# Two attention entries on TensorE: the scheduler's order against source order, with half-steps between single projection units

## The chip, the core and the metric

The kernel runs on one core of one Trainium2 chip. The metric is device time in microseconds (us) of one execution, as the median of several. TensorE (PE) multiplies matrices, with weight loads (PEld) that overlap it; VectorE (DVE), ScalarE (ACT) and GpSimd (POOL) work on its results, and SyncE (SP) issues most DMAs. Each engine takes its instructions in order and waits on semaphores for the others.

## The reference

One encoder layer is applied to two request groups with the same weights: a prompt of 1024 tokens and a sample of 512 tokens, width 1024. Cut to what matters here:

```python
h = rms_norm(x, norm_g) * (1.0 + scale) + shift
rq, rk, rv, rg, aq, ak, av, ag = jnp.split(h @ w_in, splits, axis=-1)
# (A) chunkwise retention on rq, rk, rv (4 heads of 128)
# (B) attention: 8 query heads, 2 key/value heads of 64
aq = axial_rope(rms_norm(aq, q_norm_g), ...)
ak = axial_rope(rms_norm(ak, k_norm_g), ...)
p = softmax(q @ k.T / 8)          # every query sees every key of its group
att_out = p @ v
mixed = concat([ret_out * silu(rg), att_out * silu(ag)]) @ w_out
y = x + gate * mixed
```

Everything is float32, and the products that need it are made of three matmuls on high and low parts.

## The kernel before, in words

`sequence(r, nt, first)` (from L316) handles one group. It is called for the sample first (tile names with s, `nt` = 4 tiles of 128 tokens, `first` true), then for the prompt (names with p, `nt` = 8). In each it transposes and scales the inputs into a high part `hh` and a low part `hl`, projects and computes the four retention heads, projects keys, values and the first part of the queries (`kvq_units`, L431), and then enters attention.

**Projections.** `project` (L355) makes one token tile of a query projection out of 8 times `mm3` (L148): three matmuls of 128x256, on lines 149 to 151. `q_unit` (L405) is a pair of such tiles, 48 matmuls in one PSUM bank (tile `paq`), with a yield after the first 24, and then the work of the others on it: square on ACT (`qsq`, L414), sum (`qss`), rotary (`qt1` L380, four pieces `qt2` L387) on DVE, reciprocal root and sum on POOL (`r_q` L127, `qt1` L425), and the normalised queries `q` on DVE (L401, `q_finish`, one unit later). `q_rest` (L891) yields the units that are still missing when attention starts: for the sample one pair of units and then the gates (`gates`, L760, tiles `pag`, 24 matmuls of 128x512 each with a yield in the middle); for the prompt six units of 48 matmuls (`paqp03`, `paqp13`, then `paqp00`, `paqp10`, `paqp01`, `paqp11`; the first digit is the half of the heads, the second the pair of tokens).

**Attention** is written as steps for each tile of 128 queries:

- `prep_split` (L832) splits the queries into `Q1`, on ACT and DVE for the first tile and on POOL for the others; `prep_T` (L839) transposes them (8 transposes, tile `pq1`) and ACT copies them to `Q1T` (L847).
- Row maxima: `nat_head` (L851, sample) or `nat_pairs` (L858, prompt) multiply queries by keys (tiles `pn`) and DVE reduces them to `nm` (L856) or `nmh` (L869, 128x1024, eight a tile). `mid` joins them, `mid_t` (L883) transposes them (`pnm`) and DVE writes them as extra rows of `Q2T` (L887), whose other rows are copies of low parts (`fill_q2`, L871).
- Scores: `st_unit` (L913) makes a 128x1024 score tile `pT` from `Q1T` (L910) and `Q2T` (L921), ACT takes its exponential `p` (L924), and POOL or DVE adds it to the row sums `acc` (L929, L932).
- `pv_pair` (L934) multiplies two exponentials by the values into `po`, one bank that is held for the whole tile; `row_sums` (L949), `normalise` (L957), `gate_out` and `out_step` (L1004) finish a tile; the last makes the output product `py` from `w_out`, which `read_wo` (L900) loads back from DRAM.

**Rounds.** `at_round` (L1026) files each step under a round number and a priority in it; a tile has `nt` rounds, and steps that prepare it are filed in the rounds ahead of its own. `run_rounds_list` (L271) gives a flat list of the steps of a stretch of rounds.

**Order around the change.** The rest of attention, from round `turn` on, is written inside `tc.manual_schedule` for TensorE (L1103): there the source order is TensorE's order. The entry before it, rounds -100 to `turn`, is woven in with the missing projections by `weave` (L279): after each yield of a projection it issues as many attention steps as keep the two lists in proportion, `lead` shifts that proportion. This part stands outside the manual schedule, so a scheduler with its own timing model chooses the final order on every engine. For the prompt the entry is cut at round `PTURN`: the first part runs beside `paqp03` and `paqp13`, then the half of `hh` and `hl` that is done is released and its memory goes to `Q2T`, the exponentials and the rest.

**PSUM** has eight banks. In attention the prompt has three wide buffers of two banks (`pq1`, `pn`, `pT`, `pnm`, the row sums) and two single banks (`paq`, `po`, `py`); the sample has two wide ones and four single banks.

Of the kernel before, what the change touches and what calls it, by code (L numbers as in the profile page):

```python
# [33 lines left out]
OUTLAG = 0  # L34
WZ = 2
WOH = (0,1,3,4)
LEAD = 5
PLEAD = 3
PTURN = -7
KPOST = (1, 1)  # L40
PBUFS = (5, 6)
NATS = (1, 3, 5, 6)
# [38 lines left out]
def hybrid_layer_kernel(ctx: ExitStack, tc: tile.TileContext, a: dict, y_prompt: bass.AP, y_sample: bass.AP):  # L81
# [189 lines left out]
    def run_rounds_list(rounds, lo, hi):  # L271
        return [fn for rd in sorted(rounds) if lo <= rd < hi for _, fn in sorted(rounds[rd], key=lambda z: z[0])]

    def iter_steps(fns):
        for fn in fns:
            fn()
            yield
# [38 lines left out]
    def sequence(r, nt, first):  # L316
# [4 lines left out]
        with ExitStack() as sctx:  # L321
# [11 lines left out]
            hpair = nt // 4  # L333
            tps = list(range(hpair, 2 * hpair)) + list(range(hpair))
            order = [2 * tp + i for tp in tps for i in range(2)]
            kv = {}
            QPRE = hpair if first else 1
# [160 lines left out]
            with ExitStack() as rctx:  # L498
# [292 lines left out]
                prev = None  # L791
# [47 lines left out]
            def prep_T(t):  # L839
                d = st8[t]  # L840
                Q1 = d["Q1"]
                pq = wide(f"pq1{tg}{t}")
                for h in range(QH):
                    T.transpose(pq[:, h * P : (h + 1) * P].bitcast(F32R), Q1[:, h, :, :].rearrange("p a d -> p (a d)"),
                                identr)
                d["Q1T"] = ate.tile([P, QH, P], F32R, tag="Q1T", name=f"Q1T{tg}{t}", bufs=2)
                S.copy(d["Q1T"].rearrange("p h q -> p (h q)"), pq)  # L847
                d["nm"] = ate.tile([P, QH], F32R, tag="nm", name=f"nm{tg}{t}")
                d["nmh"] = ate.tile([P, 2, QH], F32, tag="nmh", name=f"nmh{tg}{t}") if ng > 1 else None
# [8 lines left out]
            def nat_pairs(t, v, n, prev):  # L858
                d = st8[t]
                pairs = (2 * v, 2 * v + 1)  # L860
                pns = [wide(f"pn{tg}{t}{pr}{n}") for pr in pairs]
                for pn, pr in zip(pns, pairs):
                    for i in range(2):
                        rows = slice(i * DH, (i + 1) * DH)
                        T.matmul(pn[:, i * 512 : (i + 1) * 512], d["Q1T"][rows, 2 * pr + i, :],  # L865
                                 kk[v][rows, n * 512 : (n + 1) * 512], start=True, stop=True)
                for pn, pr in zip(pns, pairs):
                    with tc.issue_after(prev["mid"].ins) if "mid" in prev else ExitStack():
                        V.tensor_reduce(d["nmh"][:, n, 2 * pr : 2 * pr + 2], pn.rearrange("p (i k) -> p i k", i=2), AX.X, ALU.max, negate=True)  # L869
# [156 lines left out]
            def at_round(rd, prio, fn):  # L1026
                rounds.setdefault(rd, []).append((prio, fn))

            for n, t in enumerate(order):
                b = n * per_  # L1030
                hb = b - per_
                prev = st8[order[0]] if n == 1 else {}
                if n:
                    at_round(hb - nt // 2, 8, lambda t=t: prep_split(t))
                    at_round(hb - 1, 6, lambda t=t: prep_T(t))
                if nt == 4:
                    for h in range(QH):
                        at_round(hb + h // 2, 4, lambda t=t, h=h, prev=prev: nat_head(t, h, prev))
                else:
                    for j, k in enumerate(NATS):  # L1040
                        at_round(hb + k, 4, lambda t=t, j=j, prev=prev: nat_pairs(t, j // 2, j % 2, prev))
                for v in range(2):
                    at_round(b - 2 + v, 7.5, lambda t=t, v=v: fill_q2(t, v))
                    at_round(b - nt // 2 if v == 0 else b - 1, 7, lambda t=t, v=v: mid(t, v))
                    at_round(b - 1 + v, 3.5 if v else 5, lambda t=t, v=v: mid_t(t, v))
                for u in range(nt):
                    at_round(b + u, 1, lambda t=t, u=u: st_unit(t, u))
                    if u % 2:
                        at_round(b + u + 1, 3, lambda t=t, u=u: pv_pair(t, u // 2))
                at_round(b + per_, 3.2, lambda t=t: row_sums(t))  # L1050
                at_round(b + per_, 8.5, lambda t=t: normalise(t))
                at_round(b + per_ + 1, 9, lambda t=t: gate_out(t))
                if t == final:
                    at_round(b + per_ - 2, 9, lambda t=t: gate_ret(t))
                    at_round(b + per_ + 1, 10, lambda: final_steps(0))
                    at_round(b + per_ + 2, 10, lambda: final_steps(4))
                    continue
                for u in range(16):
                    rd = b + per_ + 3 + u * nt // 16
                    at_round(rd if first else min(rd, nt * per_), 2 if rd < nt * per_ or first else 4, lambda t=t, u=u: out_step(t, u))  # L1060
# [8 lines left out]
            for j in range(8):  # L1069
                at_round(turn + j // 2, 6, lambda j=j: read_wo(j))  # L1070

            pools["q2"] = ate
            with ExitStack() as bctx:
                ra = run_rounds_list(rounds, -100, turn)
                if first:
                    pools["at"] = sctx.enter_context(pool(f"at{tg}", bufs=2, reuse_waits="tile"))
                    pb = bctx.enter_context(pool(f"pb{tg}", bufs=2, reuse_waits="tile"))
                    prep_split(order[0])
                    prep_T(order[0])
                    weave(itertools.chain(q_rest(pb, tps[hpair], hpair), gates(pb, "tg")), 4 * (nt // 2 - QPRE) + 8 * ng,  # L1080
                          iter_steps(ra), len(ra), LEAD)
                else:
                    nb = sum(len(rounds[rd]) for rd in rounds if rd < PTURN)
                    with pool(f"pb0{tg}", bufs=2, reuse_waits="tile") as pb:
                        prep_split(order[0])
                        prep_T(order[0])
                        weave(q_rest(pb, tps[QPRE], hpair - QPRE), 4 * (hpair - QPRE), iter_steps(ra[:nb]), nb + 1)
                    hpools.pop().release()
                    pools["q2"] = sctx.enter_context(pool(f"q2{tg}", bufs=1, reuse_waits="tile"))
                    pools["at"] = sctx.enter_context(pool(f"at{tg}", bufs=2, reuse_waits="tile"))  # L1090
                    pb = bctx.enter_context(pool(f"pb{tg}", bufs=2, reuse_waits="tile"))
                    weave(q_rest(pb, tps[hpair], hpair), 4 * hpair, iter_steps(ra[nb:]), len(ra) - nb, PLEAD)
                if first:
                    ln_tables()
            for p_ in reversed(hpools):
# [37 lines left out]
```

## Time and profile before

| | us |
|---|---|
| median of 3 runs | 983.63 (981.81 to 984.15) |
| profiled execution, its own time | 980.19 |
| its span, first to last instruction | 978.3 |
| PE busy in the span | 931.1 (95%) |
| DVE / ACT / POOL busy | 545.0 / 337.1 / 348.7 |

The profile is one execution, and around its span lie 1.9 us. TensorE is the engine with little idle time, and its mean granted clock over the span is 0.983 of the full one. The share of busy time says little about one stage, so the entries are read from stretches of a few microseconds and from timelines of each engine.

### The profile page before, as it was taken

To read this page: it belongs to the slowest core of one execution; us is meant where nothing else is said; L and a number is where in the kernel's file an instruction comes from. 1 tells how busy PE (TensorE), PEld (TensorE's weight loads), DVE (VectorE), ACT (ScalarE), POOL (GpSimd) and SP (SyncE) were. 2 spreads that over 40 slices of the span, in tenths; PEclk is the share of its full clock that TensorE was granted. 3 is DMA by queue.
4 is the path that set the end of the run, shared out by engine and by line. 5 is a ranking of instruction groups with operands and counts; after the bars stand their busy time and mean duration, and the time that the engine had idled before them with its cause. 6 is when DMAs were issued, how large, how long until landed. Compare 5 with 4: busy or idle time off the path is not lost. (4 is left out here: it accounts for less than half of the span.)

```text
span 978.3 us, 15472 instructions
## 1 busy us (share of the span) xinstructions
PE 931.1 (95%) x6177; PEld 755.2 (77%) x6177; DVE 545.0 (56%) x1006; ACT 337.1 (34%) x582; POOL 348.7 (36%) x312
## 2 busy tenths in 40 slices
PE   4879998999999899999999999999899999999998
PEld 3769898987566799999999988899554555555556
DVE  2465556675664493534435343445866767676743
ACT  3352233343544362122222232232233443344341
POOL 4233453464234282222212111155442434342330
PEclk9999999999999999999999999999798999999999
DMA  9964877322821621111101111200035001101111
GB/s 274 274 185 138 269 220 248 84 58 102 363 88 44 204 66 45 44 45 44 44 14 33 43 44 44 74 2 17 0 155 210 22 22 43 44 22 44 44 44 43
DMA packets 95684, 92.99 MB, mean 95 GB/s; under 512 B 23502, under 2 KB 84858, under 8 KB 92540
## 3 DMA queue, kind: packets, MB, share of 16 engines
q1 hardware_dynamic: 92876, 77.85, 25.9%
q0 software_dynamic: 2736, 14.16, 3.7%
q8 instruction: 48, 0.79, 0.4%
q14 instruction: 24, 0.20, 0.1%
HBM read 77.30 MB, written 14.68 MB: 94 GB/s over the span
## 5 line engine op out<-in xcount | busy, mean ns | idle before, releaser
L932 POOL TENSOR_TENSOR accp<-accp,pp 128x512 f32<-128x512 f32 x48 | 64.6, 1345 | 131.9 <-ACT pp L924 130.0
L924 ACT ACTIVATE pp<-pTp 128x1024 f32<-128x1024 f32 x64 | 65.7, 1026 | 129.8 <-PE pTp L921 114.2
L869 DVE TENSOR_REDUCE nmhp<-pnp 128x2 f32<-128x1024 f32 x64 | 76.7, 1219 | 10.2 <-PE pnp L865 10.0
L941 PE MATMUL pop<-pp,VVp 128*64 128x512 f32 x256 | 66.2, 640 | 0.0
L149 PE MATMUL pvgp<-wvgp,hhp 128*128 128x256 f32 x224 | 65.1, 291 | 0.0
L149 PE MATMUL pqkp<-wqkp,hhp 128*128 128x256 f32 x224 | 64.7, 289 | 0.0
L150 PE MATMUL pvgp<-wvgp,hhp 128*128 128x256 f32 x224 | 64.4, 287 | 0.0
L151 PE MATMUL pvgp<-wvgp,hlp 128*128 128x256 f32 x224 | 63.9, 285 | 0.0
L151 PE MATMUL pqkp<-wqkp,hlp 128*128 128x256 f32 x224 | 63.7, 285 | 0.0
L150 PE MATMUL pqkp<-wqkp,hhp 128*128 128x256 f32 x224 | 63.4, 283 | 0.0
L932 DVE TENSOR_TENSOR accp<-accp,pp 128x512 f32<-128x512 f32 x48 | 34.3, 715 | 40.3 <-ACT pp L924 40.0
L149 PE MATMUL pyp<-wo,Mhp 128*128 128x512 f32 (+1 forms) x136 | 51.8, 381 | 0.0
L150 PE MATMUL pyp<-wo,Mhp 128*128 128x512 f32 (+1 forms) x136 | 51.6, 379 | 0.0
L151 PE MATMUL pyp<-wo,Mlp 128*128 128x512 f32 (+1 forms) x136 | 51.5, 379 | 0.0
L910 PE MATMUL pTp<-Q1Tp,kkp 128*128 128x512 f32 x128 | 47.7, 455 | 0.2 <-DVE nmhp L869 0.2
L921 PE MATMUL pTp<-Q2Tp,k2p 68*128 68x512 f32 x128 | 44.0, 426 | 3.5 <-DVE Q2Tp L887 3.5
L149 PEld LDWEIGHTS pqkp<-wqkp,hhp 128*128 128x128 f32 x224 | 43.0, 192 | 0.0
L150 PEld LDWEIGHTS pqkp<-wqkp,hhp 128*128 128x128 f32 x224 | 43.0, 192 | 0.0
L151 PEld LDWEIGHTS pqkp<-wqkp,hlp 128*128 128x128 f32 x224 | 42.9, 192 | 0.0
L149 PEld LDWEIGHTS pvgp<-wvgp,hhp 128*128 128x128 f32 x224 | 42.9, 191 | 0.0
L150 PEld LDWEIGHTS pvgp<-wvgp,hhp 128*128 128x128 f32 x224 | 42.8, 191 | 0.0
L151 PEld LDWEIGHTS pvgp<-wvgp,hlp 128*128 128x128 f32 x224 | 42.8, 191 | 0.0
(458 smaller groups left out, 2764.2 us busy)
## 6 DMA issues: line engine op xcount, KB each, us to landing
wo<-wod SPq DMA_DIRECT2D x16, 1024.0 KB, 14.8
wa<-in_w_ada_dram SPq DMA_DIRECT2D x16, 512.0 KB, 6.2
wod<-woz POOLq DMA_DIRECT2D x8, 1024.0 KB, 6.4
gr<-in_w_ada_dram SPq DMA_DIRECT2D x16, 256.0 KB, 5.1
xn<-in_x_prompt_dram SPq DMA_DIRECT2D x8, 512.0 KB, 6.9
xrp<-in_x_prompt_dram SPq DMA_DIRECT2D x8, 512.0 KB, 3.5
out_dram<-xrp POOLq DMA_DIRECT2D x7, 512.0 KB, 2.9
xs<-in_x_sample_dram SPq DMA_DIRECT2D x4, 512.0 KB, 6.3
```

What stands on the lines that cost most here:

```text
L149: T.matmul(out, lh, rh, start=first, stop=False)
L150: T.matmul(out, lh, rl, start=False, stop=False)
L151: T.matmul(out, ll, rh, start=False, stop=last)
L869: V.tensor_reduce(d["nmh"][:, n, 2 * pr : 2 * pr + 2], pn.rearrange("p (i k) -> p i k", i=2), AX.X, ALU.max, negate=True)
L910: T.matmul(pT[:, i * 512 : (i + 1) * 512], kk[v][:, kb], st8[t]["Q1T"][:, hs, :].rearrange("p h q -> p (h q)"), start=True, stop=False)
L921: T.matmul(pT[:, i * 512 : (i + 1) * 512], k2[v][:, kb], d["Q2T", v].rearrange("p h q -> p (h q)"), start=False, stop=True)
L924: d["exp", u] = S.activation(p, pT, AF.Exp)
L932: d["sum", v] = E.tensor_tensor(acc, acc, p[:, i * 512 : (i + 1) * 512], op=ALU.add)
L941: m = T.matmul(d["po"][v * DH : (v + 1) * DH, :], VV[:, 2 * kp + i, v, :], ps[v][:, i * 512 : (i + 1) * 512], start=(kp + i == 0), stop=(2 ...
```

## The change

The two attention entries are put inside the manual schedule for TensorE, so their source order holds there. The attention steps of an entry are no longer a flat list but go by whole rounds: `iter_rounds` yields once after all steps of a round, and `weave` alternates such half-steps with single yields of the projections. `prep_T` of the first tile becomes the first half-step. The first tile's row maxima are filed one round apart (`k if n else j`), and the three constants of the proportion are set anew.

```diff
@@ -34,9 +34,9 @@
-LEAD = 5
-PLEAD = 3
-PTURN = -7
+LEAD = 3
+PLEAD = 0
+PTURN = -2
@@ -1038,7 +1038,7 @@
                     for j, k in enumerate(NATS):
-                        at_round(hb + k, 4, lambda t=t, j=j, prev=prev: nat_pairs(t, j // 2, j % 2, prev))
+                        at_round(hb + (k if n else j), 4, lambda t=t, j=j, prev=prev: nat_pairs(t, j // 2, j % 2, prev))
@@ -1069,27 +1069,34 @@
+            def iter_rounds(lo, hi, before=()):
+                for fn in before:
+                    fn()
+                    yield
+                for rd in sorted(rounds):
+                    if lo <= rd < hi:
+                        for fn in run_rounds_list(rounds, rd, rd + 1):
+                            fn()
+                        yield
+
             pools["q2"] = ate
-            with ExitStack() as bctx:
-                ra = run_rounds_list(rounds, -100, turn)
+            with tc.manual_schedule(engines={mybir.EngineType.PE}), ExitStack() as bctx:
                 if first:
                     pools["at"] = sctx.enter_context(pool(f"at{tg}", bufs=2, reuse_waits="tile"))
                     pb = bctx.enter_context(pool(f"pb{tg}", bufs=2, reuse_waits="tile"))
                     prep_split(order[0])
-                    prep_T(order[0])
                     weave(itertools.chain(q_rest(pb, tps[hpair], hpair), gates(pb, "tg")), 4 * (nt // 2 - QPRE) + 8 * ng,
-                          iter_steps(ra), len(ra), LEAD)
+                          iter_rounds(-100, turn, [lambda: prep_T(order[0])]), nt + turn + 1, LEAD)
                 else:
-                    nb = sum(len(rounds[rd]) for rd in rounds if rd < PTURN)
                     with pool(f"pb0{tg}", bufs=2, reuse_waits="tile") as pb:
                         prep_split(order[0])
-                        prep_T(order[0])
-                        weave(q_rest(pb, tps[QPRE], hpair - QPRE), 4 * (hpair - QPRE), iter_steps(ra[:nb]), nb + 1)
+                        weave(q_rest(pb, tps[QPRE], hpair - QPRE), 4 * (hpair - QPRE),
+                              iter_rounds(-100, PTURN, [lambda: prep_T(order[0])]), nt + PTURN + 1)
                     hpools.pop().release()
...
-                    weave(q_rest(pb, tps[hpair], hpair), 4 * hpair, iter_steps(ra[nb:]), len(ra) - nb, PLEAD)
+                    weave(q_rest(pb, tps[hpair], hpair), 4 * hpair, iter_rounds(PTURN, turn), turn - PTURN, PLEAD)
```

Outside the two entries TensorE's order is the same in both kernels, and so is SP's. Three places in the prompt's entry show how the order moves (a number behind an underscore is a buffer's). First, TensorE at the transposes of the first tile's queries, tile 4; before, with the 48 matmuls of `paqp03` and 18 of `paqp13` ahead of them since the last keys:

```order
L149 MATMUL paqp13_7249<-wqp1_6961,hhp1_3519 128x256
L150 MATMUL paqp13_7249<-wqp1_6961,hhp1_3519 128x256
L151 MATMUL paqp13_7249<-wqp1_6961,hlp1_3521 128x256
L844 MATMUL pq1p4_7163<-identr_65,Q1p4_7160 128x128 x8
L149 MATMUL paqp13_7249<-wqp1_6961,hhp1_3519 128x256
```

and now, with the first 24 matmuls of `paqp03` ahead:

```order
L151 MATMUL paqp03_7176<-wqp0_6656,hlp1_3524 128x256
L844 MATMUL pq1p4_7201<-identr_65,Q1p4_7165 128x128 x8
L865 MATMUL pnp400_7214<-kkp0_6628,Q1Tp4_7210 128x512 x2
L865 MATMUL pnp410_7215<-kkp0_6628,Q1Tp4_7210 128x512 x2
L149 MATMUL paqp03_7176<-wqp0_6656,hhp1_3522 128x256
```

The transposes stand 42 projection matmuls earlier, and the first row maxima, which stood behind all of `paqp10`, follow them directly. Second, DVE at the extra rows of tile 4 (`nmhp4` are its row maxima, `Q2Tp40` its second operand for the scores); before:

```order
L401 TENSOR_TENSOR qp0_7334<-qt1p10_7452,r_qp10_7462 128x2x256
L869 TENSOR_REDUCE nmhp4_7175<-pnp430_7487 128x2
L419 TENSOR_REDUCE qssp01_7597<-qsqp01_7595 128x8
L380 TENSOR_TENSOR qt1p01_7598<-paqp01_7506,Cp00_7327 128x512
L869 TENSOR_REDUCE nmhp4_7175<-pnp421_7494 128x2
L869 TENSOR_REDUCE nmhp4_7175<-pnp431_7495 128x2
L887 TENSOR_TENSOR Q2Tp40_7502<-pnmp40_7531,identr_65 4x512
```

and now:

```order
L387 TENSOR_TENSOR qt2p13_7344<-paqp13_7278,Sp06_7170 128x8x16 x4
L401 TENSOR_TENSOR qp3_7175<-qt1p13_7342,r_qp13_7352 128x2x256
L419 TENSOR_REDUCE qssp00_7450<-qsqp00_7448 128x8
L875 COPY Q2Tp40_7401<-Q1Tp4_7210 64x2x128
L887 TENSOR_TENSOR Q2Tp40_7401<-pnmp40_7404,identr_65 4x512
L875 COPY Q2Tp41_7421<-Q1Tp4_7210 64x2x128
L380 TENSOR_TENSOR qt1p00_7451<-paqp00_7376,Cp00_7368 128x512
```

The extra rows stood right behind the last row maxima of their tile; now the maxima are long done and the rows stand behind the sum `qssp00` of a projection unit. Third, TensorE between `paqp01` and `paqp11`; before, from the end of `paqp01` on:

```order
L865 MATMUL pnp430_7487<-kkp1_6626,Q1Tp4_7172 128x512 x2
L865 MATMUL pnp421_7494<-kkp1_6626,Q1Tp4_7172 128x512 x2
L865 MATMUL pnp431_7495<-kkp1_6626,Q1Tp4_7172 128x512 x2
L886 MATMUL pnmp40_7531<-identr_65,nmp4_7174 4x128
L844 MATMUL pq1p5_7534<-identr_65,Q1p5_7483 128x128 x8
L910 MATMUL pTp40_7551<-Q1Tp4_7172,kkp0_6625 128x512 x2
L921 MATMUL pTp40_7551<-Q2Tp40_7502,k2p0_6627 128x512 x2
L886 MATMUL pnmp41_7560<-identr_65,nmp4_7174 4x128
```

and now:

```order
L151 MATMUL paqp01_7573<-wqp0_6656,hlp0_3523 128x256
L910 MATMUL pTp45_7673<-Q1Tp4_7210,kkp1_6629 128x512 x2
L921 MATMUL pTp45_7673<-Q2Tp41_7421,k2p1_6631 128x512 x2
L865 MATMUL pnp520_7682<-kkp1_6629,Q1Tp5_7416 128x512 x2
L865 MATMUL pnp530_7683<-kkp1_6629,Q1Tp5_7416 128x512 x2
L149 MATMUL paqp11_7690<-wqp1_6964,hhp0_3521 128x256
```

Before, two score tiles, two more maxima and the first value product stand between these rows and `paqp11`, all without a projection; now four rows of attention do. In the sample's entry ScalarE runs the last gate's tanh and the table load (L307) ahead of the exponential of the first tile's last score tile, `ps23`, and not behind it.

## Rows read from the trace of the kernel before

**Rows 1.** The page, first part: busy us (share of the span) xinstructions.

```profile
PE 931.1 (95%) x6177; PEld 755.2 (77%) x6177; DVE 545.0 (56%) x1006; ACT 337.1 (34%) x582; POOL 348.7 (36%) x312
```

**Rows 2.** Stretches, prompt's entry: us, then PE PEld DVE ACT POOL busy, PEclk, DMA, GB/s.

```profile
690.00:695.00 5.00, 4.09 (x29) 2.95 (x27) 5.00 (x10) 0.60 (x1) 1.28 (x1) 1.00 0.00 0
695.00:700.00 5.00, 2.40 (x12) 2.02 (x13) 4.94 (x9) 0.92 (x1) 2.62 (x4) 0.65 0.00 0
700.00:705.00 5.00, 4.65 (x13) 2.09 (x12) 4.25 (x7) 2.14 (x3) 3.58 (x3) 0.50 0.00 0
705.00:710.00 5.00, 5.00 (x12) 1.59 (x11) 2.27 (x3) 1.02 (x1) 1.99 (x2) 0.50 0.00 0
...
725.00:730.00 5.00, 4.00 (x24) 2.02 (x20) 5.00 (x9) 1.92 (x5) 4.46 (x5) 1.00 0.99 413
730.00:735.00 5.00, 4.82 (x12) 1.70 (x14) 4.94 (x7) 3.09 (x4) 4.92 (x4) 0.56 1.00 423
735.00:740.00 5.00, 4.27 (x13) 1.10 (x9) 3.77 (x6) 2.65 (x4) 0.64 (x1) 0.75 1.02 429
740.00:745.00 5.00, 4.66 (x14) 2.03 (x14) 3.72 (x5) 1.76 (x3) 0.88 (x1) 0.66 1.01 418
```

**Rows 3.** Timeline of PE: start, us, engine, line, out<-in, count [idle before <-releaser].

```profile
697.82 1.23 PE L844 MATMUL pq1p<-identr,Q1p 128*128 128x128 f32 x8 [2.19 <-DVE nmhp L869]
```

**Rows 4.** Timeline of PE, DVE and ACT: the first tile's queries in the prompt's entry.

```profile
660.70 0.68 PE L149 MATMUL paqp<-wqp,hhp 128*128 128x256 f32 x1
...
665.40 0.69 DVE L401 TENSOR_TENSOR qp<-qt1p,r_qp 128x512 f32<-128x512 f32 x1 [2.88 <-POOL r_qp L127]
...
666.18 0.62 ACT L139 CAST Q1p<-qp 128x512 fp32r<-128x512 f32 x1 [4.30 <-DVE qp L401]
...
666.84 0.69 DVE L140 TENSOR_TENSOR Q1p<-qp,Q1p 128x512 fp32r<-128x512 f32 x1 [0.74 <-ACT Q1p L139]
...
669.01 0.80 PE L844 MATMUL pq1p<-identr,Q1p 128*128 128x128 f32 x8
...
669.84 1.01 ACT L847 CAST Q1Tp<-pq1p 128x1024 fp32r<-128x1024 f32 x1 [2.13 <-PE pq1p L844]
```

**Rows 5.** Timeline of PE and DVE: pieces of a projection unit and of row maxima.

```profile
661.46 0.28 PE L149 MATMUL paqp<-wqp,hhp 128*128 128x256 f32 x1
661.58 0.28 PE L150 MATMUL paqp<-wqp,hhp 128*128 128x256 f32 x1
...
712.58 0.73 PE L865 MATMUL pnp<-kkp,Q1Tp 64*128 64x512 f32 x4
...
718.88 0.73 PE L910 MATMUL pTp<-Q1Tp,kkp 128*128 128x512 f32 x2
...
676.16 0.67 DVE L419 TENSOR_REDUCE qssp<-qsqp 128x8 f32<-128x512 f32 x1
...
677.35 0.87 DVE L387 TENSOR_TENSOR qt2p<-paqp,Sp 128x128 f32<-128x128 f32 x4
...
688.14 2.35 DVE L869 TENSOR_REDUCE nmhp<-pnp 128x2 f32<-128x1024 f32 x2
```

**Rows 6.** Timeline of PE, then stretches (PE busy, PEclk, DMA, GB/s): a wait amid projections.

```profile
159.13 0.49 PE L739 MATMUL pos<-R1s,qd1s 128*128 128x128 f32 x2 [3.04 <-DVE qd1s L716]
...
161.00:162.00 1.00, 1.00 (x7) 0.50 0.74 201
...
164.00:165.00 1.00, 1.00 (x11) 0.99 0.97 352
```

**Rows 7.** A stretch of the sample's attention, columns as in rows 2.

```profile
285.00:290.00 5.00, 3.71 (x17) 2.65 (x16) 1.97 (x3) 1.84 (x4) 2.49 (x4) 1.00 0.33 108
```

**Rows 8.** Timeline of PE: the prompt's first output product.

```profile
746.46 0.40 PE L149 MATMUL pyp<-wo,Mhp 128*128 128x512 f32 x1
```

**Rows 9.** Timeline of PE and ACT: end of the sample's entry.

```profile
247.99 0.73 PE L910 MATMUL pTs<-Q1Ts,kks 128*128 128x512 f32 x2 [0.79 <-DVE Q2Ts L887]
...
246.92 1.28 ACT L307 ACT_TABLE_LOAD   x1
```

## The prediction

> **What bounds the kernel now.** I read the page's first part, then busy time in short stretches around both attention entries, then the timelines of TensorE, VectorE, ScalarE and POOL there. TensorE is busy 95% of the span [rows 1], so only two things can be won: time in which it waits, and time in which its granted clock is at the lower of its two levels (0.50, which is 1.2 GHz). The entry of the second attention is the place that has both. In the stretches of [rows 2] the busy column falls short of 5.00 by 0.91, 2.60, 0.35 and 0 (690 to 710) and by 1.00, 0.18, 0.73 and 0.34 (725 to 745): 6.1 us of idle. The clock column costs, as busy time times one minus the clock, 0.84 + 2.33 + 2.50 = 5.7 us in the first four stretches and 2.12 + 1.07 + 1.58 = 4.8 us in the last three. Together the entry holds 6.1 + 10.5 = 16.6 us over what its matmuls need at the full clock. The cause of the first half is seen in [rows 3]: TensorE has spent its projections, holds row-maximum matmuls only, and waits 2.19 us on VectorE, which reduces them. The first attention's entry has one wait worth a name, and it comes below; nearly all of the case is the second one.
>
> **The change, part by part.** The matmuls, and the work of the other engines, are the same in number; the order is what moves. So the sum is: idle and clock loss of before, 16.6 us, against those of the new order. I walk TensorE from 660.70 on, where the first unit of the remaining projections starts [rows 4] and everything ahead is unmoved. Units are half as long as they are in the code of before: 24 matmuls, 0.12 us apart [rows 5], 2.9 us, and then a piece of attention.
>
> *The first wait.* The transposes of the first tile's queries now stand behind 24 matmuls and no longer behind 66. The 24 end near 660.70 + 0.52 + 23 x 0.12 = 664.1 (the first of a kind takes some 0.5). But the queries come off a chain that the change leaves where it was: normalisation on VectorE at 665.40, ScalarE's high part at 666.18, VectorE's low part at 666.84 for 0.69 [rows 4]. TensorE waits until 667.5: **3.4 us**. Before, the transposes came at 669.01 and found the queries ready. Then the row maxima follow at once and need the transposed copy, which ends 1.84 us after the first transpose (669.01 to 669.84 + 1.01) and is handed over some 0.06 later; the eight transposes take 0.80 of that: **1.1 us**.
>
> *PSUM buffers.* Three wide buffers turn round. The fourth row-maximum tile waits for the reduction of the third, 1.13 us (two take 2.35 with overlap) plus a hand-over of some 0.25, and has two tiles, 0.73 us, ahead of it [rows 5]: 0.6. One score tile waits likewise for an exponential of 1.01 and has two maximum tiles ahead of it, 0.4. **1.0 us**.
>
> *The first scores.* On VectorE the copy and the maximum row of Q2Tp40 now stand behind qssp00, which needs ScalarE's square of a unit whose last matmul is the one just ahead of the scores. After that matmul: a 128x512 pass of ScalarE (0.62), qssp00 (0.6), a copy (between 0.2 and 0.69, I take 0.2), the row (0.69) and hand-overs, 2.3 us, of which TensorE fills 0.5 with the first score pair: **1.8 us**.
>
> *The last bank.* From the first value product on, one of the two small banks is held by pop4, so paqp11 needs the bank of paqp01. Its release is 0.62 on ScalarE, then 1.2 for two VectorE passes (676.16 to 677.35), 1.13 for a reduction that stands between them, 0.8 for four rotary pieces [rows 5], and 0.25: 4.0 us. TensorE has a score tile (two pairs like that of 0.73, some 1.0 with overlap) and two maximum tiles (0.73) to do: **2.3 us**.
>
> *The end of the entry.* After the last projection the order is that of before, tile 5 without any output projection to fill it. The last unit's square, sum and rotary now stand ahead of both maximum rows of tile 5 on VectorE, and pnp610 waits for a reduction behind tile 4's normalisation. I walk 0.8 + 0.4 + 1.75 = **2.95 us**; bounds are the 2.25 that before has there [rows 2] and 4.
>
> New idle: 3.4 + 1.1 + 1.0 + 1.8 + 2.3 + 2.95 = 12.6 us.
>
> *The clock.* No row shows this order, so I bound it. The nearest row to the first wait is a wait of 3.04 us amid dense projections in the first sequence [rows 6]: there the clock then stood at 0.50 for some three us and was back at 164, since dense work followed. That is 1.7 us, and I take it, because 24 dense matmuls follow here too; the upper bound is the 5.7 us of [rows 2], where sparse work followed, the lower is 0. For the middle waits I take 0: 1.29 us of idle left the clock at 1.00 [rows 7]. For the end I take half of the 4.8 us, between 0 and 4.8. Sum 4.1 us.
>
> The Trainium skill ("TensorE: Matmul & The Clock Gate", section "A second HAM failure mode: psum-queue depth-cycling") speaks against this reading: a TensorE that idles briefly but often between groups, as it turns through PSUM banks, falls to its lower clock and comes back again and again. The stretch of [rows 7] does not show that for one such wait, and no stretch of before has as many in a row as the new order; by that rule the sum would be some 5 us higher, three waits at 1.7 us each (third rival).
>
> Second entry: 12.6 + 4.1 - 16.6 = +0.1 us.
>
> *Loads.* The eight loads of the split w_out go out behind the last projection, which by the walk ends near 729, and move with it, as do the DMAs behind them on SP's queue. In [rows 2] the DMA share stands near 1.00 for 20 us, 2.5 us a load. The first product that needs one stood at 746.46 [rows 8]; it has over ten us of cover left, and later loads are needed slower than they come. Nothing. If that cover went, each microsecond would be lost in full.
>
> *First entry.* At most the wait of 0.79 us goes [rows 9]. But ScalarE now runs the last gate's tanh (0.62, a 128x512 pass) and the table load (1.28) ahead of the exponential (1.01, the 128x1024 pass of [rows 4]) whose buffer the next transposes need: 2.9 us, of which TensorE covers some 1.5. I take +0.4, between -0.8 and +0.6. The early moves of POOL's and VectorE's pieces (the second tile's split, Q2Ts copies) lie beside projections and cost nothing while those last; without that cover they would be late by their own 0.6 to 1.3 us.
>
> Total: +0.1 + 0.4 = **+0.5 us**. Against the profiled execution of 980.19 that is 980.7; the median of the three runs, 983.63, is 3.4 above that execution, so I give **984.1**. Within 0.3% (2.95 us) is about what a measurement here can't tell from no change.
>
> **The rivals.**
> 1. *The clock stays up.* Projections mixed in are just what [rows 2] lacked. If neither the first wait nor the end stage loses clock, the second entry is 12.6 - 16.6 = -4.0, total -3.6: **980.0**. For it: every stretch with projections has clock 1.00. Against it: the first wait is longer than the 3.04 us that did lower the clock. It decides if the granted clock is 1.00 from 730 on and lower for under two us near 667.
> 2. *The first wait costs as [rows 2] did.* After it come transposes, a second wait and row maxima before the 24 matmuls, so the half clock may hold for the 13 us that it held from 696 to 710: 5.7 us in place of 1.7, total +4.5: **988.1**. It decides if the clock is still 0.50 when paqp13 starts (about 677).
> 3. *Every bank wait lowers the clock.* Three middle waits (scores, buffer, last bank) at 1.7 us each: total +5.6, **989.2**. The skill's rule above would have it so; of the rows only [rows 3] has a 2 us wait with a fall, and it stood amid sparse work.
> That the order does not come out as written is excluded: it is read from the built program.
>
> **How the numbers follow.** Forecast, no change that can be told: 0.47. Rival 1: 0.26. Rival 2: 0.21. Rival 3: 0.06. The forecast's own range is from 981 to 987 by the bounds of the end stage and of the first entry. To hold 8 in 10 the range reaches past rival 1 by a microsecond of shorter waits and just past rival 2: 979.0 to 988.7. Faster 0.26, same 0.47, slower 0.27.
>
> **What would show it.** A wait of 3 to 3.5 us before the first tile's transposes near 664, released by VectorE's low part, with the clock at 0.50 in the next stretch; about 1.8 us before Q2Tp40's scores, 2.3 before paqp11; the stretch that was 695 to 710 without a clock below 0.9; the first output product of tile 4 within 2 us of 746.5; in the first entry about 1.5 us before the transposes, released by ScalarE. I am wrong in kind if the first tile's transposes do not wait, or if the first output product comes before 743 or after 750.

## The result and the profile after

The changed kernel takes **989.13 us** (median of 15 runs, 984.37 to 993.79), the kernel before 984.12 (15 runs, 976.52 to 988.82). The ratio is 1.0055 with a 95% interval of 1.0033 to 1.0077, so the change costs 5.4 us (3.2 to 7.6) where the prediction said +0.5. It lies outside the range and on the slower side.

The work is the same and TensorE is still what bounds it. First part of the page of the changed kernel, as [rows 1] (busy us, share of the span, instructions):

```profile
PE 930.5 (94%) x6177; PEld 758.3 (77%) x6177; DVE 546.9 (55%) x1006; ACT 336.9 (34%) x582; POOL 349.5 (35%) x312
```

TensorE's busy time is within 0.6 us of before and the span is 987.0 instead of 978.3. To see where the 8.7 us come from, the span is cut at rows that both traces have, and only three pieces differ. The **first entry** runs from the gate broadcast of the sample (L392) to its first output product (L149), the **second entry** likewise in the prompt, and the **boundary** from the prompt's first zero product (L517), where the sample's work is over, to the first `pqkp` projection.

| stretch, us | before | changed |
|---|---|---|
| first entry | 59.4 | 62.0 |
| boundary | 37.2 | 40.1 |
| second entry | 87.1 | 90.9 |

Each piece of the rest is equal within 0.4 us. The boundary will turn out not to be the change's; the two entries are. Timeline of TensorE in the changed kernel, its waits (start, us, engine, line, out<-in, count, idle before and its releaser):

```profile
201.44 0.38 PE L149 MATMUL paqs<-wqs,hhs 128*128 128x256 f32 x1 [0.67 <-ACT gates L393]
...
248.94 0.51 PE L844 MATMUL pq1s<-identr,Q1s 128*128 128x128 f32 x4 [1.66 <-ACT ps L924]
...
667.24 0.39 PE L149 MATMUL paqp<-wqp,hhp 128*128 128x256 f32 x1 [0.68 <-ACT gmod L393]
...
673.01 0.84 PE L844 MATMUL pq1p<-identr,Q1p 128*128 128x128 f32 x8 [2.63 <-DVE Q1p L140]
674.95 0.80 PE L865 MATMUL pnp<-kkp,Q1Tp 64*128 64x512 f32 x2 [1.10 <-ACT Q1Tp L847]
...
681.87 0.50 PE L865 MATMUL pnp<-kkp,Q1Tp 64*128 64x512 f32 x2 [0.86 <-DVE nmhp L869]
...
698.49 1.07 PE L921 MATMUL pTp<-Q2Tp,k2p 68*128 68x512 f32 x2 [2.30 <-DVE Q2Tp L887]
...
726.75 0.55 PE L149 MATMUL paqp<-wqp,hhp 128*128 128x256 f32 x1 [2.50 <-DVE qt2p L387]
...
741.10 0.73 PE L910 MATMUL pTp<-Q1Tp,kkp 128*128 128x512 f32 x2 [0.39 <-ACT pp L924]
742.34 0.73 PE L921 MATMUL pTp<-Q2Tp,k2p 68*128 68x512 f32 x2 [0.51 <-DVE Q2Tp L887]
...
751.05 0.50 PE L865 MATMUL pnp<-kkp,Q1Tp 64*128 64x512 f32 x2 [1.50 <-DVE nmhp L869]
...
755.49 0.39 PE L149 MATMUL pyp<-wo,Mhp 128*128 128x512 f32 x1
```

The waits that the prediction walked are all here, where it put them and nearly as long (the second entry starts 5.3 us later than in [rows 4], so 673.01 is 667.7 in the time of before). Two rows were not expected, those at 201.44 and 667.24. Stretches of one microsecond in the second entry (PE busy and its instructions, PEclk, DMA share, GB/s):

```profile
674.00:675.00 1.00, 0.05 (x2) 0.86 0.00 0
675.00:676.00 1.00, 1.00 (x4) 0.50 0.00 0
...
678.00:679.00 1.00, 1.00 (x10) 0.93 0.06 16
...
698.00:699.00 1.00, 0.51 (x2) 0.81 0.00 0
699.00:700.00 1.00, 1.00 (x5) 0.50 0.06 16
...
702.00:703.00 1.00, 1.00 (x10) 0.98 0.00 0
...
726.00:727.00 1.00, 0.25 (x1) 0.50 0.00 0
727.00:728.00 1.00, 1.00 (x6) 0.50 0.00 0
...
732.00:733.00 1.00, 1.00 (x4) 0.62 0.00 0
...
743.00:744.00 1.00, 1.00 (x5) 0.50 1.00 418
...
746.00:747.00 1.00, 1.00 (x6) 0.80 0.95 401
```

The clock falls to 0.50 (1.2 GHz) four times: after the first wait, after the wait for `Q2Tp40`, after the wait for the last bank and in the end stage. Busy time times one minus the clock, summed over stretches of 1 us, gives 1.6 + 1.6 + 3.0 + 1.7 = 7.9 us (8.0 with stretches that begin at the entry's own start). The last of the four stands behind two short waits, of 0.39 and 0.51 us, and none stands behind the 1.50 us wait at 751. The long fall of [rows 2] at 695 to 710 is gone, as forecast; in place of it and the two falls that before has behind it, near 730 and 740, there are four. By the same sums the second entry of before has 6.1 us idle and 11.0 of clock loss, the changed one 13.3 and 8.0: +4.2, against the 3.7 by which the stretch grew.

### The profile page after: what moved, and what is told of

Same layout as the page of the kernel before. It is cut to its first block, busy times and chain, and to the rows that moved or that the text cites. A ratio compares the mean times of both kernels' runs of the same rounds, so it can differ in the third digit from the quotient of the medians.

```text
span 987.0 us, 15467 instructions
## 1 busy us (share of the span) xinstructions
PE 930.5 (94%) x6177; PEld 758.3 (77%) x6177; DVE 546.9 (55%) x1006; ACT 336.9 (34%) x582; POOL 349.5 (35%) x312
## 5 line engine op out<-in xcount | busy, mean ns | idle before, releaser
L149 PE MATMUL pvgp<-wvgp,hhp 128*128 128x256 f32 x224 | 65.0, 290 | 0.0
L149 PE MATMUL pqkp<-wqkp,hhp 128*128 128x256 f32 x224 | 64.6, 288 | 0.0
L941 PE MATMUL pop<-pp,VVp 128*64 128x512 f32 x256 | 63.7, 619 | 0.0
L932 DVE TENSOR_TENSOR accp<-accp,pp 128x512 f32<-128x512 f32 x48 | 34.2, 712 | 37.4 <-ACT pp L924 37.1
L149 PE MATMUL pyp<-wo,Mhp 128*128 128x512 f32 (+1 forms) x136 | 51.8, 381 | 0.0
L910 PE MATMUL pTp<-Q1Tp,kkp 128*128 128x512 f32 x128 | 45.6, 438 | 0.8 <-ACT pp L924 0.8
L149 PEld LDWEIGHTS pqkp<-wqkp,hhp 128*128 128x128 f32 x224 | 43.0, 192 | 0.0
L149 PEld LDWEIGHTS pvgp<-wvgp,hhp 128*128 128x128 f32 x224 | 42.8, 191 | 0.0
```

The lines of the kernel that those rows point to most:

```text
L149: T.matmul(out, lh, rh, start=first, stop=False)
L910: T.matmul(pT[:, i * 512 : (i + 1) * 512], kk[v][:, kb], st8[t]["Q1T"][:, hs, :].rearrange("p h q -> p (h q)"), start=True, stop=False)
L932: d["sum", v] = E.tensor_tensor(acc, acc, p[:, i * 512 : (i + 1) * 512], op=ALU.add)
L941: m = T.matmul(d["po"][v * DH : (v + 1) * DH, :], VV[:, 2 * kp + i, v, :], ps[v][:, i * 512 : (i + 1) * 512], start=(kp + i == 0), stop=(2 ...
```

## The experiments

The table gives for each run the three stretches of its profiled execution, idle and clock loss in the second entry summed in the same way, and the ratio to the kernel before on the same chip.

| run | first | boundary | second | idle + clock | ratio (95%) |
|---|---|---|---|---|---|
| before | 59.4 | 37.2 | 87.1 | 6.1 + 11.0 | 1 |
| changed | 62.0 | 40.1 | 90.9 | 13.3 + 8.0 | 1.0055 (1.0033 to 1.0077) |
| e1 sample only | 61.9 | 38.6 | 86.2 | 7.1 + 9.0 | 1.0026 (1.0000 to 1.0052) |
| e2 prompt only | 59.4 | 39.6 | 92.4 | 13.4 + 9.5 | 1.0050 (1.0023 to 1.0077) |
| e3 wide first | 61.1 | 37.7 | 90.5 | 13.3 + 7.9 | 1.0054 (1.0030 to 1.0078) |
| e4 one unit later | 62.0 | 39.6 | 86.3 | 10.6 + 6.6 | 0.9996 (0.9969 to 1.0022) |
| e5 spread | 63.0 | 39.2 | 83.3 | 8.8 + 4.7 | 0.9957 (0.9933 to 0.9981) |
| e6 late value products | 62.0 | 37.0 | 85.5 | 9.6 + 6.6 | 0.9995 (0.9973 to 1.0016) |
| e7 transposes ahead | 61.0 | 37.8 | 90.6 | 13.4 + 7.9 | 1.0068 (1.0040 to 1.0096) |
| e8 mix | 59.4 | 39.2 | 76.8 | 5.3 + 1.7 | 0.9869 (0.9840 to 0.9899) |
| e9 before, late value products | 59.3 | 38.9 | 79.6 | 5.2 + 3.4 | 0.9913 (0.9884 to 0.9942) |
| e10 mix, wide first | 61.4 | 37.9 | 77.9 | 5.1 + 3.3 | 0.9911 (0.9879 to 0.9943) |
| e11 changed again | 64.5 | 38.6 | 89.7 | 13.4 + 6.5 | 989.42 us, one execution |
| e12 before again | 59.4 | 37.1 | 88.9 | 6.5 + 12.4 | 981.72 us, one execution |

**One entry at a time (e1, e2).** The block under `pools["q2"] = ate` exists twice, once as in the change and once as before, and `first` chooses:

```diff
-            with tc.manual_schedule(engines={mybir.EngineType.PE}), ExitStack() as bctx:
+            if first:
+                with tc.manual_schedule(engines={mybir.EngineType.PE}), ExitStack() as bctx:
...
+            else:
+                with ExitStack() as bctx:
+                    ra = run_rounds_list(rounds, -100, turn)
...
```

with the constants of each side (e2 has the two branches the other way round).

> New order in the first attention's entry only; the second entry has the code and the constants of before. Three stretches are read: first entry (gate broadcast of the sample, line 392, to its first output product, line 149; 59.4 us before, 62.0 in the changed kernel), boundary (first xTp transposes of the prompt's loading to its first pqkp projection; 36.8 and 39.6), second entry (gate broadcast of the prompt to its first output product; 87.1 and 90.9). Theory A (each entry loses by itself, the boundary differs from run to run): first entry 62.0, second 87.1, time about +2.6 us over before. Rival B (a later sample makes the boundary's transfers land later, so the boundary's 2.8 us belong to the change): boundary 39.6 here, time about +5.5 us. Rival C (the second entry is where it is lost): time within 1 us of before.

> New order in the second attention's entry only; the first entry has the code and the constant of before. Theory A: first entry 59.4 us, second 90.9, time about +3.7 us over before; the clock falls to 0.50 after the wait for Q2Tp40 and after the wait of the last bank as in the changed kernel. Rival B: the boundary stays at 36.8 here and time is +3.7 as well, so that this run and the one before it differ by the boundary. Rival C (all is lost in the first entry): time within 1 us of before.

Each entry loses by itself: +2.6 us (2.5 in the first entry's stretch; the interval of the time begins at 0) and +4.9 us (5.2 in the second's). The clock did not fall after the wait for `Q2Tp40` in e2, against its expectation. The boundary is 38.6 and 39.6, so it goes with neither side. e11 and e12 are the two kernels themselves, profiled once more:

> The changed kernel itself, profiled a second time, to tell what belongs to its order and what to one execution. If the fall of the clock after the wait for Q2Tp40 belongs to the order, the clock is at 0.50 after that wait here too; if it is the execution's, as the runs with the same order suggest, it may stay at 1.00 there, and the fall after the first wait lasts some seven us in its place. Under both the idle of the second entry is 13.3 us within 0.3, its clock loss 7.9 to 9.5, and the fall after the wait for the last bank is there. If the boundary belongs to the change it is 40.1 us again, if to the execution anything from 37 to 40.

> The kernel before, profiled a second time. If the boundary belongs to the change it is 37.2 us again; if to the execution, anything from 37 to 40. The second entry is 86 to 88 us with some 6 us of idle and 9 to 11 us of clock loss, the first entry 59.4.

What TensorE waits for at the boundary (engine, line, waited for: us in total, times, longest), in the kernel before:

```profile
PE p0p L149 <- ACT hhp L507: 3.5, 1, 3.5
```

in the changed kernel:

```profile
PE p0p L149 <- ACT hhp L507: 6.3, 1, 6.3
```

and in e11, the same kernel again:

```profile
PE p0p L149 <- ACT hhp L507: 4.7, 1, 4.7
```

In both kernels' first profiles ScalarE's `hhp` is released by the landing of the sample's last output DMA, in e11 by that of a weight load (`wvgp0r`). One kernel shows 4.7 and 6.3, and kernels with the first entry of before show 37.1 to 39.6 for the stretch. Over all 14 profiles it is 37.0 to 40.1 with no order that goes with the change. So the 2.8 us of the profiled pair are mostly one execution's. e11 missed one expectation: its clock loss is 6.5, below 7.9; and its first entry is 64.5 (below). e12 missed one too: its second entry is 88.9 with 12.4 us of clock loss, over 86 to 88 and 9 to 11. So the order of before has a second entry of 86.2 to 88.9 us (before, e1, e12), the new one 89.7 to 92.4 (changed, e2, e3, e7, e11). The ranges do not meet, and the means lie 3.4 us apart; e2's 5.2 is the difference of one pair of profiles.

**The first projection's bank (e3).**

```diff
-                pq = wide(f"pq1{tg}{t}")
+                pq = st8[t].get("pq") or wide(f"pq1{tg}{t}")
...
                     prep_split(order[0])
+                    st8[order[0]]["pq"] = wide(f"pq1{tg}{order[0]}")
```

(the second line stands in both entries).

> Changed kernel, but the wide PSUM buffer of the first tile's transposes is allocated before the projections' first bank, as in before; the transposes stand where the change puts them. Theory A (the first remaining projection waits for ScalarE's copy of the gate broadcast only because its bank is now the one of that broadcast): the 0.7 us wait after line 392 goes in both entries; the first entry is 1.0 us shorter (61.0), the second as long as it was (90.9), since the projection that starts earlier only waits longer for Q1p4 (2.6 becomes some 3.8). Rival D (the swap of banks is the whole of the loss, because it also makes the middle waits): first entry 59.4 and second 87.1. Rival E (nothing but the place of the wait changes): both as in the changed kernel.

Theory A held. With `prep_T` as a half-step, the projections' `bank` tiles are the first to be allocated in the new pool, and they get the banks of the gate broadcast, which ScalarE has yet to copy. In e3 these waits are gone and the first entry is 0.9 us shorter. The second entry stays, since its next wait takes the time over. TensorE's waits in e3's second entry:

```profile
PE pq1p L844 <- DVE Q1p L140: 3.5, 1, 3.5
PE pTp L921 <- DVE Q2Tp L887: 2.9, 3, 2.2
PE paqp L149 <- DVE qt2p L387: 2.6, 2, 2.5
```

The wait for `Q1p4` is 3.5 instead of 0.68 + 2.63.

**What else the first entry loses (e7).** On top of e3:

```diff
-                    at_round(hb - 1, 6, lambda t=t: prep_T(t))
+                    at_round(hb - 1, 0.9 if first and n == 2 else 6, lambda t=t: prep_T(t))
```

> Changed kernel with the wide buffer allocated first (as in the third run), and in the first entry the transposes of the third tile's queries stand ahead of the last score pair of the first tile, so that their buffer no longer hangs on the exponential behind the tanh and the table load. Theory A (that order on ScalarE is what the first entry still loses): the 1.66 us wait before these transposes goes and at most 0.8 us comes back at the next buffer, first entry 60 us against 61.1. Rival H (tanh, table load, exponential and copy are one chain on ScalarE and TensorE meets its end in any order): the wait stands before pTs30 or pnms30 instead, first entry 61 or more. Second entry as in the third run, 90.5.

Rival H held: 61.0 us. ScalarE in the changed kernel (timeline):

```profile
245.86 0.60 ACT L362 ACTIVATE tg_as<-pags 128x512 f32<-128x512 f32 x1 [3.81 <-PE pags L151]
246.48 1.28 ACT L307 ACT_TABLE_LOAD   x1
247.77 1.02 ACT L924 ACTIVATE ps<-pTs 128x1024 f32<-128x1024 f32 x1
```

This chain begins when the last gate's projection ends, and TensorE meets its end in whatever it does next. In e3 the wait was the 1.7 us before the transposes, in e7 it is split (TensorE's waits in e7):

```profile
PE pnms L886 <- ACT Q1Ts L847: 0.9, 1, 0.9
PE pTs L910 <- ACT ps L924: 0.7, 1, 0.7
```

The 1.66 us wait can also cost clock. In e1, e5 and e11 the granted clock stands at 0.50 after it (1.7, 1.7 and 3.4 us of loss), in the changed kernel's first profile, e3, e4 and e6 it does not. That is the 64.5 of e11 (stretches of 5 us):

```profile
249.00:254.00 5.00, 4.46 (x16) 0.56 1.01 426
254.00:259.00 5.00, 5.00 (x19) 0.75 1.01 428
```

**More ahead of the transposes (e4, e5).** e4 gives the second entry's first `weave` a lead of one unit; e5 deals its six half-steps out as 0, 1, 2, 3 behind the four units:

```diff
-                              iter_rounds(-100, PTURN, [lambda: prep_T(order[0])]), nt + PTURN + 1)
+                              iter_rounds(-100, PTURN, [lambda: prep_T(order[0])]), nt + PTURN + 1, 1)
```

```diff
+            def batches(it, sizes):
+                for k in sizes:
+                    for _ in range(k):
+                        next(it, None)
+                    yield
...
-                              iter_rounds(-100, PTURN, [lambda: prep_T(order[0])]), nt + PTURN + 1)
+                              batches(iter_rounds(-100, PTURN, [lambda: prep_T(order[0])]), (0, 1, 2, 3)), 4)
```

> Changed kernel, but the first half-step of the second entry stands behind 48 projection matmuls and not behind 24. Theory A (the wait for Q1p4 and the clock that falls after it are paid because there is too little ahead of the transposes): 24 matmuls are 2.9 us, the wait of 2.6 us before the transposes goes to under 0.5 and no stretch at 0.50 follows; of the 2.6 + 1.6 us some 2 to 4 come back, second entry 87 to 89 us. Rival F (the cover is only moved: the matmuls taken forward are missing at the later waits, which grow by as much): second entry 90 to 92. If the middle waits stay above 2 us the clock falls after each of them here too.

> Changed kernel, but the six half-steps of the second entry's first part are dealt out as 0, 1, 2 and 3 behind its four projection units, where the changed kernel has 2, 2, 1 and 1 and the run with one unit more ahead had 0, 3, 2 and 1. Theory A (waits come from half-steps that follow each other at once): the transposes find Q1p4 ready, the 1.1 us for the copy of Q1Tp4 lie beside 24 matmuls, and no wait of the first part reaches 1 us, so no stretch there stands at 0.50; with the wait for Q2Tp40 gone as in that run, the second entry takes 82 to 84 us, against 90.9 and 86.3. Rival F (cover is only moved): the row maxima that come later make the row for Q2Tp40 late, a wait of 2 us or more stands before the first score pair again and the clock falls after it: 86 to 88 us.

Theory A's mechanism held in both: 86.3 (4.6 under the changed kernel, and under the 87 to 89 expected) and 83.3 (7.6 under it). In e4 the wait for `Q1p4` is gone, and with it that for `Q2Tp40`, which drops from 2.3 to at most 0.5; but row maxima now follow each other at once and one waits 1.9 us. Behind it the clock falls after all (1.7 us of loss), where Theory A expected no such stretch. TensorE's longest waits in e4, then a stretch:

```profile
PE pnp L865 <- DVE nmhp L869: 4.6, 3, 1.9
PE paqp L149 <- DVE qt2p L387: 2.6, 2, 2.5
PE pnp L865 <- ACT Q1Tp L847: 1.1, 1, 1.1
...
679.00:680.00 1.00, 1.00 (x5) 0.50 0.07 16
```

In e5 the first part has no wait of 1 us and no stretch below 1.00; the last bank's wait of 2.5 us is left, and the clock falls after it.

**The last bank (e6, e8, e9).** The value products of the prompt's first tile, and with them its accumulator, move behind the start of the last projection unit:

```diff
-                        at_round(b + u + 1, 3, lambda t=t, u=u: pv_pair(t, u // 2))
+                        late = not first and not n
+                        at_round(b + (6, 7, 8, 8)[u // 2] if late else b + u + 1, 0.5 if late and u < 7 else 3,
+                                 lambda t=t, u=u: pv_pair(t, u // 2))
```

e6 is this edit on the changed kernel. e8 has the first entry of before, and in the second both edits, e5's and this one.

> Changed kernel, but the value products of the second entry's first tile start in round 6 (pairs in rounds 6, 7, 8 and 8, ahead of the round's scores, instead of 2, 4, 6 and 8), so that the last projection bank is taken before their accumulator is. Theory A (the wait before paqp11 is for a bank that the accumulator keeps, and its clock loss is a part of the middle waits): the 2.5 us wait goes, with it the 2.7 us of clock in 725 to 735, and the products that are left for the end stage fill its 1.5 us wait for a reduction: second entry 85 to 87 us. Rival G (TensorE is held by VectorE's total work in the entry, whichever wait shows it): other waits on VectorE grow, second entry 89 or more. The wait for Q2Tp40 (2.3 us) and the fall after it stay as they were under both.

> First entry with the code and the constant of before, second entry with both edits of this group (half-steps dealt out 0, 1, 2, 3; value products from round 6). If theory A holds for both edits and they add up: first entry 59.4 us, second entry 79 to 82, time 5 to 8 us under before. If rivals F or G hold, the second entry is 85 or more and the time within 2 us of before.

e6 gives 85.5: the wait is gone, and so is the 1.5 us wait of the end stage, for which waits of 1.0 and 0.7 us come, with a longer fall of the clock behind them (3.4 us of loss, against 1.7). The wait for `Q2Tp40` stayed at 2.2 us, but the clock did not fall after it, against what both theories expected. e8 beats both kernels: 969.53 us (967.76 to 970.11), 12.9 us under before by the ratio, where 5 to 8 were expected, with a second entry of 76.8, below the 79 to 82 expected. TensorE's waits there, from 658 to 760 us:

```profile
PE pnp L865 <- DVE nmhp L869: 1.7, 2, 0.9
PE pTp L921 <- DVE Q2Tp L887: 1.2, 2, 1.0
PE pnp L865 <- ACT pp L924: 0.7, 1, 0.7
PE paqp L149 <- ACT gmod L393: 0.7, 1, 0.7
PE pTp L921 <- ACT Q2Tp L875: 0.6, 1, 0.6
PE pTp L910 <- ACT pp L924: 0.5, 1, 0.5
```

No wait is over 1.0 us, and yet one fall of the clock is left (1.7 us, near 731). It stands behind two waits of 0.99 and 0.69 us in a row. Whether the late value products need the new order at all was asked of the kernel before, with that edit alone:

> The kernel before with one edit, the one on the value products (from round 6). It asks whether that edit is good by itself or only in the new order. Theory A: in the order of before no projection waits for the accumulator's bank, since nearly all projections are spent before the first scores; there is nothing to remove, the waits for VectorE and the long stretch at 0.50 amid scores stay, second entry 86 to 89 us (87.1 before), time within 2 us of before. Rival G (late value products as such, as fill for the end stage, bring the gain of the runs with that edit): second entry 83 or less.

**Theory A failed here.** The second entry falls to 79.6 and the time by 8.5 us. I had read the order of before as one whose projections are simply spent. But with the accumulator `pop4` allocated later, `paqp11` takes the bank of `paqp10`, which is free early, and its 48 matmuls, which stood behind the first value product, come between and behind the row maxima (they start at 695.20, and the last rotary piece on `paqp01` ends at 700.9). So in the order of before `pop4` had that bank. The other one, that of `paqp01`, was free there at 700.4, when its last rotary piece ended, and `paqp11` came only at 710.25, behind the first value product. Why the scheduler put it so far behind the bank is not shown. Stretches in e9, whose second entry starts 1.8 us later than in [rows 2]:

```profile
695.00:700.00 5.00, 5.00 (x35) 1.00 0.00 0
700.00:705.00 5.00, 4.96 (x37) 1.00 0.30 77
705.00:710.00 5.00, 4.55 (x20) 1.00 1.02 429
...
725.00:730.00 5.00, 4.75 (x17) 0.57 0.04 16
```

The 2.19 us wait of [rows 3] and the fall at 695 to 710 are gone. Rival G's number (83 or less) was right, though not by filling the end stage: the gain lies before 710. So an accumulator that is allocated early cost both kernels, before through sparse work, the changed one through the 2.5 us wait.

> The mixed kernel of the last group (first entry of before, second entry with both edits) with the wide buffer of the first tile's transposes allocated first in the second entry too. The 0.7 us wait of the first projection for ScalarE's copy goes. Theory A: the 48 matmuls then end some 1.2 us earlier, at about the time at which Q1p4 is ready, so that up to 1.0 us of wait for it appears in its place: second entry 76 to 77 us (76.8 without). Rival: the wait reappears with a fall of the clock, 78 or more.

e10 is e8 with e3's line in the second entry. The 0.7 us went and 0.6 us before the transposes came, as expected; the end stage's fall lasted longer (3.3 us of loss), so that the second entry of 77.9 lies between the two theories, and its first entry, the same program as in e8, is 61.4 through a wait of 1.6 us that e8 has at 0.3. It is not shown to be better or worse than e8 by its edit.

## Why the prediction was wrong

- *Idle of the second entry.* Right in its parts. Predicted 12.6, measured 13.3. First wait 3.4 (0.68 + 2.63), copy 1.1 (1.10), buffers 1.0 (0.86 + 0.45), first scores 1.8 (2.30), last bank 2.3 (2.50, and 0.16 once before), end stage 2.95 (0.39 + 0.51 + 0.23 + 1.50 = 2.6). Two readings behind it were off: 660.70 + 0.52 + 23 x 0.12 is 663.98 and not 664.1, which changes nothing, and at [rows 3] TensorE had not spent its projections, since the 48 matmuls of `paqp11` were still to come (e9).
- *The clock.* This step failed: "For the middle waits I take 0". They cost 1.6 (the first scores) and 3.0 us (the last bank) in the first profile, and nothing behind the buffers. The sum was to be 4.1 and is 8.0, and in all profiles with the changed kernel's second entry (changed, e2, e3, e7, e11) 6.5 to 9.5. The row that it rested on, 1.29 us of idle at a clock of 1.00 [rows 7], was too short for waits of 2 us and more; the wait of 3.04 us [rows 6] was the nearer one. And [rows 2] itself holds falls behind short waits. Near 730 and 740 the clock of before falls behind rows that waited at most 0.95 us:

```profile
728.77 0.22 PE L886 MATMUL pnmp<-identr,nmp 128*4 128x128 f32 x1 [0.95 <-DVE nmhp L869]
...
740.18 0.50 PE L865 MATMUL pnp<-kkp,Q1Tp 64*128 64x512 f32 x2 [0.68 <-ACT pp L924]
```

The first wait was taken at 1.7 and cost 1.6, but 3.2 in e2, e3, e6 and e7.
- *First entry.* This step failed too. Predicted +0.4 and at most +0.6, measured +2.6 (2.5 in e1, 5.1 in e11). "Everything ahead is unmoved" was wrong for one instruction: the first remaining projection lost its free bank, which e3 prices at 0.9 us (in the second entry it hid in the first wait). The wait for ScalarE was walked as 1.5 and is 1.66, but I counted only part of it against the 0.79 us [rows 9] that go; the difference is 0.9. That it can lower the clock was not priced. Of e3's 61.1 against 59.4, 1.3 us are idle; the other 0.4, without a wait, is not explained.
- *Loads, output products.* The loads were right: they run at a DMA share near 1.00 from 740 on and no product waits for them. The first output product was not: it was to come within 2 us of 746.5, and 750 was named as the time past which the forecast is wrong in kind. It came at 755.49, 9.0 us later than before, 3.7 after taking off the later start. Most of what it came late over the forecast is the clock's (8.0 us for 4.1).
- *The rivals.* Rival 1 is out: the clock is at 0.50 at 743. Rival 2 gave 988.1, but its mechanism is out too: the first wait cost 1.6 to 3.2 us of clock and not 5.7. Rival 3 gave 989.2 and had a chance of 0.06. Its time was met, its mechanism half: in all seven profiles with the last bank's wait the clock fell after it, after the wait for `Q2Tp40` in two of six, after the 0.86 us wait for a buffer in none. Its price of 1.7 us each was too high for one and too low for another. The rest of the time came from the first entry, which no rival had. The Trainium skill ("TensorE: Matmul & The Clock Gate", section "A second HAM failure mode: psum-queue depth-cycling") has a TensorE that idles briefly but often, as it turns through PSUM banks, fall to its lower clock again and again. The runs bear it out in the end stage: behind the waits of 0.39 and 0.51 us that follow each other there the clock fell in four of seven profiles (changed, e3, e5, e7), behind those of 1.0 and 0.7 us in all three (e6, e8, e10). Of each pair one wait is for a PSUM buffer, the other for a row of `Q2T`. A wait of 0.86 us alone cost no clock.

The experiments add that the loss could be undone piece by piece: the first wait by e4, the maxima by e5, the bank by e6. The two edits of e8 took 7.6 and 5.4 us of the second entry singly and 14.1 together, each by one profile.

## What to carry to other kernels

When work is reordered by hand, walk the buffers in the order of their allocation too: a tile allocated one step earlier or later gets another bank, and an accumulator taken early starves what is allocated behind it. A wait of TensorE is to be priced with a fall of the clock behind it, so removing it can pay twice: in the second entry every wait of 2.5 us or more had one, those of 1.5 to 2.3 us had one in some profiles, and so had pairs of waits under 1 us. Deal small dependent steps out one or two to a unit of dense work, with a full unit between a step and the one that reads its result.

## What was not expected of the hardware

With the same TensorE order around it, a wait of 2.2 to 2.3 us for `Q2Tp40` was followed by a clock of 0.50 in both profiles of the changed kernel and not in e2, e3, e6 and e7. In e2 (stretches of 1 us):

```profile
695.00:696.00 1.00, 0.00 (x0) 1.00 0.00 0
696.00:697.00 1.00, 0.27 (x1) 1.00 0.00 0
697.00:698.00 1.00, 1.00 (x9) 1.00 0.06 16
```

In e2, e3, e6 and e7 the fall after the first wait lasted some seven us (3.2 us of loss), in both profiles of the changed kernel some three (1.6). In the end stage the pair of waits of 0.39 and 0.51 us was followed by a fall in the changed kernel's first profile and not in its second, e11; there a fall came behind a wait of 1.81 us. What decides between these was not found; between e2 and the changed kernel no engine's order differs in this entry. An entry's clock loss is therefore known only to some 3 us from one profile (6.5 to 9.5 for one order).
